# GLA with two chunks at a time and a single carried state

## The chip, the core and the metric

The kernel runs on one core of a Trainium2 chip. The core's engines work from queues of their own, each in order: PE (TensorE) does matmuls, DVE (VectorE), ACT (ScalarE) and POOL (GpSimd) do elementwise work, and SP issues most DMAs; ACT's queue issues some too. The metric is the device time of one execution, in microseconds (us), the median of three runs.

## What is computed

Two layers of a mixer with three branches (attention, RWKV-7, gated linear attention) on 256 tokens of 1024 channels, all in float32. The change is in gated linear attention (GLA): four heads with keys of 128 and values of 256 channels, in chunks of 64 tokens. `cum` is the running sum of the log decay inside a chunk.

```python
q_dec = q * jnp.exp(cum)
k_inv = k * jnp.exp(-cum)
k_to_end = k * jnp.exp(cum_last - cum)
attn = jnp.einsum('bnihd,bnjhd->bnhij', q_dec, k_inv)
attn = jnp.where(jnp.tril(jnp.ones((CHUNK, CHUNK), bool)), attn, 0.0)
o_intra = jnp.einsum('bnhij,bnjhv->bnihv', attn, v)
def step(state, inp):
    q_c, k_c, v_c, d_c = inp
    o_c = jnp.einsum('bihd,bhdv->bihv', q_c, state)
    state = state * d_c[..., None] + jnp.einsum('bjhd,bjhv->bhdv', k_c, v_c)
    return state, o_c
```

The output of a head is `o_intra` plus what the steps give; it is then divided by its root mean square over the 256 values, scaled, gated by a silu of `z` and projected.

## The kernel before

**Dense products.** Nearly all of PE's time goes to products with weights of 1024 rows. A weight tile of 128 x 1024 comes by a DMA from SP, ACT casts it to a high part (`hi_..`, L344), DVE subtracts for the low part (`lo_..`, L345), and PE runs three passes of 256-column matmuls for it (`dense`, L358, result `ps_..`; `dense_tok`, L371, with tokens in the partitions). The names say which weights: `gq`, `gk`, `gv`, `gz` are GLA's queries, keys, values and gate input, `gt` is the gate of the merge, `wo` an output projection, `rk`, `rr`, `rv` RWKV's.

**The RWKV chain.** Each layer does RWKV in two halves. A half begins with `gram` products (PE L574, masked by DVE into `Gm` L581), whose result goes out and back by DMAs on ACT's queue (`bd` L591, `Bb` L596) to the triangular solve on POOL: 31 steps of a `tm` multiply (L607) and an `Xb` update (L610), strictly one after another. The result leaves by `xd` (L612) and returns as `Xs` (L616), both issued on ACT's queue. Then a chain of eight chunks runs: `u` (PE L692, reads `Xs`), `vals` (DVE L696), `sp` (L702), a state (`gst` POOL L712, `ST` DVE L716). `ptok` turns a chunk's keys, which POOL prepares in `bks` (L643, L646).

**GLA** is called behind the first half's RWKV code and runs over its solve. `gla_gates` gives `e1`, `e2`, `ke` (the exponentials of the reference) and `el` (a chunk's whole decay). In `gla`, per layer: `qd` (L833), `ki` in `e2` (L837) and `kte` in `ke` (L838) are the three decayed tensors, channels in the partitions. For each 128 tokens PE turns `kte` (`pk` L847; ACT copies it to `kt` L848) and makes `pat` = `ki`^T `qd` (L850), which DVE masks into `at` (L851) for two chunks side by side. For each head, a state `S` is carried over three chunks: `kv` (PE L868, 64 tokens in either half of the rows), a copy (L871) or multiply-add (L873) on DVE. The output `po` [128 values, 256 tokens], twice per head, is a 128-column product with `at` (L880) for 128 tokens and a 64-column product with `S` (L882) for each of the chunks 1 to 3. ACT squares `po` (`gsq` L886), DVE copies it to `og` (L887), POOL adds the two halves of `gsq` (L888), and PE sums them over channels into `gss` (L144). After all heads comes `grn` (L891), turned by PE (`ptrg`) and spread by it (`gbc`); DVE scales `og` (L901), POOL multiplies it by the gate `tz` (L903), ACT and DVE split it into `ghi` and `glo` for `wo`.

**What sets the order.** The program is written in one order, and a scheduler that works at build time lays the instructions of each engine's queue out from it; the queues run in that order. The modulation of the next part (`adaw` L263 on DVE, one weight DMA each) is interleaved with the weight tiles. Small results of PE share three buffers (`ps_m`); `gss` holds one of them from the first head to the last.

Of the kernel before, what the change touches and what calls it, by code (L numbers as in the profile page):

```python
# [10 lines left out]
F32 = mybir.dt.float32  # L11
# [4 lines left out]
ALU = mybir.AluOpType  # L16
# [18 lines left out]
# Column slots of w_in, 256 columns each (see _w_in_columns).  # L35
# [7 lines left out]
# Columns of the packed per-channel parameters, one per 128 channels.  # L43
# [6 lines left out]
# Order of the column tiles of ada_w: shift and scale of the same channels side by side.  # L50
# [11 lines left out]
def _turn_pieces():  # L62
    """frac(2^k / 2 pi) for the steps of the pieces of an angle, each as a 12-bit part and the rest."""
# [13 lines left out]
def trunk(  # L77
# [45 lines left out]
    # running sums start again at every 32nd or 64th token  # L123
# [17 lines left out]
    def sums(ps, src, sel):  # L141
        """ps [128, 2, n]: sums over channels of src [128, 256 tokens], tokens in the partitions."""
        for half in range(2):
            PE.matmul(ps[:, half], src[:, half * P:(half + 1) * P], sel, start=True, stop=True)  # L144

    def to_rows(pool, src, n, nm):
        """[2 n, 256]: src [128, 2, n], given for tokens, turned and in two parts that one pass carries."""
# [12 lines left out]
    def spread(ps, rows, j, sel):  # L160
        """ps [128 channels, 256] = row j, both parts."""
        PE.matmul(ps, sel[:, j:j + 1].broadcast_to([sel.shape[0], P]), rows, start=True, stop=True)

    def spread2(ps, rows, j):
        """Row j to the first 64 channels, the next to the others."""
# [81 lines left out]
    def interleave():  # L247
        """Part of the modulation that is wanted later, between two weight transfers."""
# [5 lines left out]
    def ada_part(L, l, slots, pool=None):  # L254
        """Two columns of the modulation for each slot, 128 channels each, before its bias."""
# [12 lines left out]
    def start(L, hl, firsts, order):  # L268
        """The first layer's input and its first products of it, 128 channels at a time as their
        modulation comes in."""  # L270
# [62 lines left out]
    def weights(src, name, n=2048, pool=None, sub=None):  # L333
        """Both parts of n columns of a slot, in tiles of CHUNK columns."""
# [14 lines left out]
    def dense(ps, w, kt, i, act):  # L349
        """ps [128 columns, 256 tokens] = W[:, column tile i].T @ activations; a tile's rows side by side."""  # L350
# [945 lines left out]
```

## Time and profile before

| what | value |
|---|---|
| three runs, us | 1183.28, 1189.07, 1191.8 (median 1189.07) |
| span of the profiled execution, us | 1181.3 |
| PE busy | 1103.1 us, 93% |
| DVE, ACT, POOL busy | 68%, 49%, 40% |
| chain that ended last, by engine | PE 58%, POOL 16%, DVE 9%, DMA 8% |

All times in rows are microseconds from the start of the span of one profiled execution, unless marked ns. A row of a timeline gives start, duration, engine, line, operation, what it writes and reads, and how often. A matmul's duration is longer than the distance to the next one, since they are pipelined; the distance is what it costs. A matmul of float32 operands is two instructions. The granted clock is a share of TensorE's full 2.4 GHz; its lower level is 1.2 GHz.

### The profile page before, as it was taken

The numbers are of one execution on the slowest core, as the hardware profiler recorded it, in microseconds if no ns is written. First come the engines' busy times: TensorE is split into PE (matmuls) and PEld (weight loads), VectorE is DVE, ScalarE is ACT, GpSimd is POOL, SyncE is SP. The second block draws the span as 40 slices with busy tenths as digits, with TensorE's granted clock in tenths as the row PEclk, the third lists the DMA queues.
The fourth block names the chain that finished last, engine by engine and source line by source line (L and its number), as shares of the span: only waits on it lengthen the run. The fifth ranks groups of instructions, "written<-read, shape, count | busy, mean of one in ns | idle before, by whom it ended". The sixth has DMA issues, their size and how long they took to land.

```text
span 1181.3 us, 25207 instructions
## 1 busy us (share of the span) xinstructions
PE 1103.1 (93%) x10365; PEld 1001.9 (85%) x10365; DVE 799.6 (68%) x1220; ACT 578.8 (49%) x980; POOL 466.6 (40%) x609
## 2 busy tenths in 40 slices
PE   5799898999999599999989999899999969999997
PEld 3798887988999477999989889789899968799997
DVE  6978754766986667677665685367677665667774
ACT  4357233545547243554556834255384635446452
POOL 7955338324536643103100536523063753211210
PEclk7799998999999899999999989999999989999999
DMA  9665753465466443547654245334444542234761
GB/s 353 215 200 167 176 154 117 131 219 153 144 220 216 128 143 103 120 151 231 207 182 150 83 153 161 107 90 133 146 141 138 181 123 91 81 120 142 249 210 40
DMA packets 70066, 185.15 MB, mean 157 GB/s; under 512 B 24608, under 2 KB 25120, under 8 KB 69824
## 3 DMA queue, kind: packets, MB, share of 16 engines
q1 hardware_dynamic: 48304, 173.37, 46.3%
q10 hardware_dynamic: 21648, 10.18, 3.4%
q8 instruction: 81, 1.33, 0.5%
q14 instruction: 33, 0.27, 0.1%
HBM read 179.32 MB, written 4.20 MB: 155 GB/s over the span
## 4 chain that ended last, share of the span: by engine, by line
PE 58%; POOL 16%; DVE 9%; DMA 8%; issue 5%; ACT 4%; ACTq 1%; DVEq 0%; SPq 0%; POOLq 0%
PE ps_gt L358 10%; PE ps_wo L358 9%; POOL tm L607 5%; POOL Xb L610 5%; PE ps_rz L358 4%; PE y L371 3%; PE ps_gz L358 3%; PE ps_gq L358 2%; PE ps_mz L358 2%; PE ps_rk L358 2%; PE ps_rv L358 2%; DMA wr_wout<-in_wout_dram 2%; DMA Bb<-bd 1%; DMA adaw<-in_ada_dram 1%; PE sp L702 1%
## 5 line engine op out<-in xcount | busy, mean ns | idle before, releaser
L358 PE MATMUL ps_gt<-hhi,lo_gt 128*128 128x256 f32 x384 | 109.9, 286 | 0.1
L358 PE MATMUL ps_gt<-hhi,hi_gt 128*128 128x256 f32 x384 | 109.7, 286 | 0.0
L358 PE MATMUL ps_gt<-hlo,hi_gt 128*128 128x256 f32 x384 | 109.0, 284 | 0.0
L345 DVE TENSOR_TENSOR lo_gt<-wr_gt,hi_gt 128x1024 fp32r<-128x1024 f32 x48 | 63.4, 1322 | 40.1 <-ACT hi_gt L344 39.6
L345 DVE TENSOR_TENSOR lo_wo<-wr_wo,hi_wo 128x1024 fp32r<-128x1024 f32 x48 | 67.2, 1399 | 31.3 <-ACT hi_wo L344 31.1
L263 DVE SCALAR_TENSOR_TENSOR adaw<-adaw,cb 128x1024 f32<-128x1024 f32 x48 | 70.7, 1476 | 15.1 <-DMA adaw<-in_ada_dram 14.8
L344 ACT CAST hi_gt<-wr_gt 128x1024 fp32r<-128x1024 f32 x48 | 50.4, 1049 | 54.9 <-PE ps_gt L358 20.1
L344 ACT CAST hi_wo<-wr_wo 128x1024 fp32r<-128x1024 f32 x48 | 50.4, 1050 | 51.0 <-PE ps_gt L358 25.1
L358 PEld LDWEIGHTS ps_gt<-hhi,lo_gt 128*128 128x128 f32 x384 | 73.4, 191 | 1.5 <-DVE lo_gt L345 0.4
L358 PEld LDWEIGHTS ps_gt<-hhi,hi_gt 128*128 128x128 f32 x384 | 73.6, 192 | 1.0 <-issue 0.2
L712 POOL TENSOR_TENSOR gst<-ST,GC 64x256 f32<-64x256 f32 x48 | 39.0, 813 | 88.8 <-DVE ST L716 75.0
L358 PEld LDWEIGHTS ps_gt<-hlo,hi_gt 128*128 128x128 f32 x384 | 73.5, 191 | 0.6 <-issue 0.2
L607 POOL TENSOR_TENSOR tm<-Xb,Bb 128x126 f32<-128x126 f32 (+22 forms) x124 | 64.8, 523 | 22.9 <-DMA Bb<-bd 13.7
L785 POOL TENSOR_TENSOR merged<-merged,tg 128x512 f32<-128x512 f32 x14 | 24.6, 1758 | 122.6 <-DVE tg L784 108.9
L610 POOL TENSOR_TENSOR Xb<-Xb,tm 128x126 f32<-128x126 f32 (+22 forms) x124 | 61.0, 492 | 9.5
L643 POOL COPY bks<-vs 128x128 f32<-128x128 f32 x32 | 11.1, 346 | 131.4 <-PE ptok L650 125.4
L654 ACT COPY vals<-ptok 32x128 f32<-32x128 f32 x128 | 32.9, 257 | 46.7 <-PE ptok L650 34.2
L344 ACT CAST hi_gz<-wr_gz 128x1024 fp32r<-128x1024 f32 x16 | 16.8, 1048 | 50.6 <-PE ps_gz L358 18.8
L696 DVE COPY vals<-u 32x128 f32<-32x128 f32 x128 | 36.5, 286 | 7.0 <-PE u L692 5.1
L371 PE MATMUL ps_gv<-hi_gv,hhi 128*128 128x256 f32 x128 | 36.5, 289 | 3.4 <-ACT hi_gv L344 2.3
L358 PE MATMUL ps_gz<-hhi,hi_gz 128*128 128x256 f32 x128 | 39.6, 309 | 0.0
L358 PE MATMUL ps_gz<-hhi,lo_gz 128*128 128x256 f32 x128 | 39.3, 307 | 0.0
(492 smaller groups left out, 4358.9 us busy)
## 6 DMA issues: line engine op xcount, KB each, us to landing
adaw<-in_ada_dram SPq DMA_DIRECT2D x48, 512.0 KB, 3.8
wr_gt<-in_win_dram SPq DMA_DIRECT2D x48, 512.0 KB, 3.9
wr_wo<-in_wo_dram SPq DMA_DIRECT2D x48, 512.0 KB, 3.8
wr_rk<-in_win_dram SPq DMA_DIRECT2D x16, 512.0 KB, 5.1
wr_rr<-in_win_dram SPq DMA_DIRECT2D x16, 512.0 KB, 4.5
wr_rv<-in_win_dram SPq DMA_DIRECT2D x16, 512.0 KB, 4.2
wr_gv<-in_win_dram SPq DMA_DIRECT2D x16, 512.0 KB, 4.4
wr_gz<-in_win_dram SPq DMA_DIRECT2D x16, 512.0 KB, 4.2
```

Source lines behind the costliest of these rows:

```text
L263: V.scalar_tensor_tensor(w, w, 0.5, cb, ALU.mult, ALU.mult, accum_out=L.mod[:, ADA_ORDER[2 * s + i]:ADA_ORDER[2 * s + i] + 1],)
L344: A.copy(hi, wr)
L345: (sub or V).tensor_sub(lo, wr, hi.bitcast(F32))
L358: PE.matmul(ps if len(a.shape) == 2 else ps.rearrange("p (a b) -> p a b", a=2), wt[:, at + k * P:at + (k + 1) * P], a, start=i == 0, stop= ...
L371: PE.matmul(ps, a[:, st * P:(st + 1) * P] if len(a.shape) == 2 else a[:, st], wt[:, k * n % CHUNK:k * n % CHUNK + n], start=i == 0, stop=i ...
L607: G.tensor_mul(tv, Xb[:, 0:nr, m:m + 1].broadcast_to([P, nr, w]), Bb[:, m:m + 1, m + 1:32].broadcast_to([P, nr, w]))
L610: G.tensor_add(Xb[:, 0:nr, m + 1:32], Xb[:, 0:nr, m + 1:32], tv)
L654: A.copy(vals[ch % 2][rows(g2, 1 - gh), :, gh, g2], pt[32 * g:32 * g + 32, 2].rearrange("p (q v) -> p q v", q=2))
L696: V.tensor_copy(val[rows(g2, gh), :, gh, g2], u[rows(g2, gh)])
L702: PE.matmul(sp[chan(qi), 2 * gh:2 * gh + 2].rearrange("p g v -> p (g v)"), tk[:, gh, chan(qi)], val[:, qi, gh].rearrange("p g v -> p (g v) ...
L712: G.tensor_mul(gst[chan(qi)], ST[chan(qi), :, qi], R.GC[chan(qi), :, ch:ch + 1].broadcast_to([64, 4, 64]))
L785: (V if b == 2 and s == 3 else G).tensor_add(m, m, tg)
```

## The change

In each 128 tokens the queries of the second chunk now read the first chunk's keys directly: `pax` (64 keys x 64 queries, from `kte` and `qd`) fills the corner of `at` that the mask left at zero, copied there by ACT. With that only one state is needed, that of the first 128 tokens at their end: `ks` holds their keys decayed to token 128 (the first chunk's times the second chunk's decay `el`), and `qs` the queries of tokens 128 to 255 (the last chunk's times the third's decay). Both are made by four new POOL operations into a tile `far`. Only `ks` is turned, `kv` is one product over 128 rows per head, `S` a copy, and `po` three 128-column products for each of its halves.

```diff
@@ -837,18 +837,33 @@
             V.tensor_mul(e2[:, g2], e2[:, g2], ps)
             V.tensor_mul(ke[:, g2], ke[:, g2], ps)
         ki, kte = e2, ke
+
+
+        el3 = el.rearrange("p (h c) -> p h c", c=4)
+        far = gp.tile([P, 2, 4, P], F32, tag="g4", name="far", bufs=6)
+        ks, qs = far[:, 0], far[:, 1]
+        G.tensor_mul(ks[:, :, 0:64], kte[:, :, 0:64], el3[:, :, 1:2].broadcast_to([P, 4, 64]))
+        G.tensor_copy(ks[:, :, 64:128], kte[:, :, 64:128])
+        G.tensor_copy(qs[:, :, 0:64], qd[:, :, 128:192])
+        G.tensor_mul(qs[:, :, 64:128], qd[:, :, 192:256], el3[:, :, 2:3].broadcast_to([P, 4, 64]))
         at = gp.tile([P, 2, 4, P], F32, tag="g4", name="at", bufs=6)
-        kt = gp.tile([P, 2, 4, P], F32, tag="g4", name="kt", bufs=6)
         for st in range(2):
             ts = slice(st * P, (st + 1) * P)
-            pk = ps_m.tile([P, 4, P], F32, tag="m", name="pk")
             pa = ps_m.tile([P, 4, P], F32, tag="m", name="pat")
-            for hd in range(4):
-                PE.transpose(pk[:, hd], kte[:, hd, ts], ident)
-            A.copy(kt[:, st], pk)
+            px = ps_m.tile([64, 4, 64], F32, tag="m", name="pax")
             for hd in range(4):
                 PE.matmul(pa[:, hd], ki[:, hd, ts], qd[:, hd, ts], start=True, stop=True)
+            for hd in range(4):
+                PE.matmul(
+                    px[:, hd], kte[:, hd, st * P:st * P + 64], qd[:, hd, st * P + 64:(st + 1) * P],
+                    start=True, stop=True)
             V.tensor_mul(at[:, st], pa, amask.unsqueeze(1).broadcast_to([P, 4, P]))
+            A.copy(at[0:64, st, :, 64:128], px)
+        kt = gp.tile([P, 4, P], F32, name="kt")
+        pk = ps_m.tile([P, 4, P], F32, tag="m", name="pk")
+        for hd in range(4):
+            PE.transpose(pk[:, hd], ks[:, hd], ident)
+        A.copy(kt, pk)
         og = [big(f"og{i}") for i in range(2)]
         ss = ps_m.tile([P, 2, 4], F32, tag="m", name="gss")
         for hd in range(4):
@@ -861,27 +876,16 @@
                     dense_tok(ps[:, st], w, KD, 256, h, st)
                 v = gp.tile([P, 2, T], F32, tag="v", name="v", bufs=2)
                 A.copy(v, ps)
-            S = [None]
-            for ch in range(3):
-                kv = ps_m.tile([P, T], F32, tag="m", name="kv")
-                r = slice(64 * (ch % 2), 64 * (ch % 2) + 64)
-                PE.matmul(kv, kt[r, ch // 2, hd], v[r, ch // 2], start=True, stop=True)
-                Sn = gp.tile([P, T], F32, tag="S", name="S", bufs=4)
-                if ch == 0:
-                    V.tensor_copy(Sn, kv)
-                else:
-                    V.scalar_tensor_tensor(Sn, S[ch], el[:, 4 * hd + ch:4 * hd + ch + 1], kv, ALU.mult, ALU.add)
-                S.append(Sn)
+            kv = ps_m.tile([P, T], F32, tag="m", name="kv")
+            PE.matmul(kv, kt[:, hd], v[:, 0], start=True, stop=True)
+            S = gp.tile([P, T], F32, tag="S", name="S", bufs=2)
+            V.tensor_copy(S, kv)
             po = ps_m.tile([P, 2, T], F32, tag="m", name="po")
             for dt in range(2):
                 dc = slice(dt * P, (dt + 1) * P)
-                for st in range(2):
-                    first = max(1, 2 * st)
-                    PE.matmul(po[:, dt, st * P:(st + 1) * P], v[:, st, dc], at[:, st, hd], start=True, stop=False)
-                    for ch in range(first, 2 * st + 2):
-                        PE.matmul(
-                            po[:, dt, 64 * ch:64 * ch + 64], S[ch][:, dc],
-                            qd[:, hd, 64 * ch:64 * ch + 64], start=False, stop=ch == 2 * st + 1)
+                PE.matmul(po[:, dt, 0:P], v[:, 0, dc], at[:, 0, hd], start=True, stop=True)
+                PE.matmul(po[:, dt, P:T], v[:, 1, dc], at[:, 1, hd], start=True, stop=False)
+                PE.matmul(po[:, dt, P:T], S[:, dc], qs[:, hd], start=False, stop=True)
             sq = small("gsq")
             A.activation(sq, po, AF.Square)
             V.tensor_copy(og[hd // 2][:, 2 * (hd % 2):2 * (hd % 2) + 2], po)
```

Some comments fall away elsewhere, without effect on the program. SP's order of DMAs is the same. The scheduler lays the queues out anew from `pat` on; three places of the new order follow, each with rows of before first. The three are of layer 0.

DVE, behind the last of `lo_gv` before the solve, before:

```order
L345 TENSOR_TENSOR lo_gv_2290<-wr_gv_2291,hi_gv_2289 128x1024
L851 TENSOR_TENSOR at<-pat,cs 128x512
L263 SCALAR_TENSOR_TENSOR adaw_0_2471,mod_1697<-adaw_0_2471,cb 128x1024
L851 TENSOR_TENSOR at<-pat,cs 128x512
L871 COPY S<-kv 128x256
L581 TENSOR_TENSOR Gm<-gram,cs 128x4x128 x2
L873 SCALAR_TENSOR_TENSOR S<-S,el,kv 128x256
L263 SCALAR_TENSOR_TENSOR adaw_0_2474,mod_1697<-adaw_0_2474,cb 128x1024
L873 SCALAR_TENSOR_TENSOR S<-S,el,kv 128x256
```

and now:

```order
L345 TENSOR_TENSOR lo_gv_2265<-wr_gv_2266,hi_gv_2264 128x1024
L860 TENSOR_TENSOR at<-pat,cs 128x512 x2
L263 SCALAR_TENSOR_TENSOR adaw_0_2434,mod_1697<-adaw_0_2434,cb 128x1024
L581 TENSOR_TENSOR Gm<-gram,cs 128x4x128 x2
L263 SCALAR_TENSOR_TENSOR adaw_0_2437,mod_1697<-adaw_0_2437,cb 128x1024
L345 TENSOR_TENSOR lo_gz_2358<-wr_gz_2359,hi_gz_2357 128x1024
L581 TENSOR_TENSOR Gm<-gram,cs 128x4x128 x2
```

Both `at` multiplies stand ahead of the first `adaw` product, and the updates of `S` are gone.

POOL, the end of the solve, before (the two rows of a step are `tm` and `Xb`):

```order
L607 TENSOR_TENSOR tm<-Xb,Bb 128x45
L610 TENSOR_TENSOR Xb<-Xb,tm 128x15x3
L607 TENSOR_TENSOR tm<-Xb,Bb 128x30
L610 TENSOR_TENSOR Xb<-Xb,tm 128x15x2
L607 TENSOR_TENSOR tm<-Xb,Bb 128x16
L610 TENSOR_TENSOR Xb<-Xb,tm 128x16
L888 TENSOR_TENSOR gsq<-gsq 128x256
L643 COPY bks<-vs_742 128x128
```

and now:

```order
L607 TENSOR_TENSOR tm<-Xb,Bb 128x45
L610 TENSOR_TENSOR Xb<-Xb,tm 128x15x3
L607 TENSOR_TENSOR tm<-Xb,Bb 128x30
L907 TENSOR_TENSOR og_2001<-og_2001,tz 128x512
L610 TENSOR_TENSOR Xb<-Xb,tm 128x15x2
L907 TENSOR_TENSOR og_2001<-og_2001,tz 128x512
L607 TENSOR_TENSOR tm<-Xb,Bb 128x16
L907 TENSOR_TENSOR og_2002<-og_2002,tz 128x512
L610 TENSOR_TENSOR Xb<-Xb,tm 128x16
L907 TENSOR_TENSOR og_2002<-og_2002,tz 128x512
L643 COPY bks<-vs_742 128x128
L646 TENSOR_TENSOR bks<-BK_744,GC_745 128x256
```

Three of the four `og` multiplies (L907, L903 before) stand between the last steps, the fourth right behind them; the `gsq` add that stood behind the solve is now in its middle, four `gsq` adds in all standing ahead of the first `og`.

PE, around the first `u`, before:

```order
L358 MATMUL ps_gz_2625<-hhi_98,hi_gz_2619 128x256
L358 MATMUL ps_gz_2625<-hlo_99,hi_gz_2619 128x256
L358 MATMUL ps_gz_2625<-hhi_98,lo_gz_2620 128x256
L153 MATMUL ptrg_2381<-cs,hlg_2378 8x128 x2
L692 MATMUL u<-zs,Xs 32x64 x8
L644 MATMUL ptok<-cs,bks 128x128
L650 MATMUL ptok<-cs,bks 128x128 x2
L358 MATMUL ps_gz_2625<-hhi_98,hi_gz_2619 128x256
L358 MATMUL ps_gz_2625<-hlo_99,hi_gz_2619 128x256
L358 MATMUL ps_gz_2625<-hhi_98,lo_gz_2620 128x256
L358 MATMUL ps_gt_2698<-hhi_98,hi_gt_2680 128x256
L358 MATMUL ps_gt_2698<-hlo_99,hi_gt_2680 128x256
```

and now:

```order
L358 MATMUL ps_wo_2787<-ghi_2350,hi_wo_2775 128x256
L358 MATMUL ps_wo_2787<-glo_2352,hi_wo_2775 128x256
L358 MATMUL ps_wo_2787<-ghi_2350,lo_wo_2776 128x256
L358 MATMUL ps_wo_2787<-ghi_2350,hi_wo_2775 128x256
L692 MATMUL u<-zs,Xs 32x64 x8
L644 MATMUL ptok<-cs,bks 128x128
L650 MATMUL ptok<-cs,bks 128x128 x2
L358 MATMUL ps_wo_2787<-glo_2352,hi_wo_2775 128x256
L358 MATMUL ps_wo_2787<-ghi_2350,lo_wo_2776 128x256
L358 MATMUL ps_wo_2787<-ghi_2349,hi_wo_2781 128x256
L358 MATMUL ps_wo_2787<-glo_2351,hi_wo_2781 128x256
```

Here `u` reads what the solve gives. 96 `gt`, 22 `wo`, four `gbc` and three more `gz` matmuls now stand ahead of it that stood behind it. In the other layer, 19 more `gz` matmuls stand ahead of the first `u`, and on POOL two of the new `far` operations stand inside the solve.

## Rows read from the trace of the kernel before

**Rows 1.** The page, busy time, share of the span and instructions of one engine:
```profile
PE 1103.1 (93%) x10365; PEld 1001.9 (85%) x10365; DVE 799.6 (68%) x1220; ACT 578.8 (49%) x980; POOL 466.6 (40%) x609
```

**Rows 2.** Windows: busy of PE, PEld, DVE, ACT, POOL; granted clock; DMA share; GB/s:
```profile
100.00:125.00 25.00, 22.94 (x186) 22.24 (x186) 24.23 (x30) 16.55 (x24) 14.95 (x12) 1.00 0.41 128
200.00:220.00 20.00, 17.15 (x142) 15.58 (x140) 9.75 (x20) 11.69 (x19) 6.54 (x16) 0.83 0.35 105
240.00:260.00 20.00, 20.00 (x247) 18.12 (x246) 13.71 (x22) 9.20 (x14) 5.26 (x6) 1.00 0.71 221
740.00:760.00 20.00, 15.67 (x116) 13.22 (x115) 6.66 (x11) 4.43 (x7) 11.96 (x27) 0.91 0.37 105
```

**Rows 3.** Waits in 139:152, 160:210 and 735:760: total us, times, longest:
```profile
PE kv L868 <- DVE at L851: 3.1, 2, 2.0
...
PE gss L144 <- POOL gsq L888: 5.2, 2, 2.8
...
PE gss L144 <- POOL gsq L888: 4.3, 1, 4.3
```

**Rows 4.** Windows, the stretch 154 to 156:
```profile
154.00:156.00 2.00, 2.00 (x59) 1.88 (x52) 2.00 (x4) 0.00 (x0) 0.00 (x0) 0.52 0.16 20
```

**Rows 5.** Timeline of PE: start, us, engine, line, operation, count, [idle before it <-releaser]:
```profile
150.51 0.70 PE L868 MATMUL kv<-v,kt 64*128 64x256 f32 x2 [2.04 <-DVE at L851]
```

**Rows 6.** Timeline of PE in both layers, pitches and groups:
```profile
164.75 0.70 PE L868 MATMUL kv<-v,kt 64*128 64x256 f32 x4
...
727.73 1.05 PE L850 MATMUL pat<-qd,e 128*128 128x128 f32 x8
728.71 0.70 PE L868 MATMUL kv<-v,kt 64*128 64x256 f32 x4
...
760.70 0.70 PE L868 MATMUL kv<-v,kt 64*128 64x256 f32 x2
761.33 0.39 PE L358 MATMUL ps_gz<-hhi,lo_gz 128*128 128x256 f32 x1
...
762.75 0.28 PE L358 MATMUL ps_gz<-hlo,hi_gz 128*128 128x256 f32 x1
...
763.90 0.49 PE L880 MATMUL po<-at,v 128*128 128x128 f32 x2
...
766.27 0.70 PE L868 MATMUL kv<-v,kt 64*128 64x256 f32 x2
```

**Rows 7.** Timeline of DVE, layer 0:
```profile
148.62 1.23 DVE L263 SCALAR_TENSOR_TENSOR adaw<-adaw,cb 128x1024 f32<-128x1024 f32 x1 [3.17 <-DMA adaw<-in_ada_dram]
```

**Rows 8.** Timeline of POOL, layer 0, in and behind the solve:
```profile
180.73 0.72 POOL L888 TENSOR_TENSOR gsq<-gsq 128x256 f32<-128x256 f32 x1
...
203.46 0.23 POOL L610 TENSOR_TENSOR Xb<-Xb,tm 128x16 f32<-128x16 f32 x1
...
214.90 0.62 POOL L646 TENSOR_TENSOR bks<-BK,GC 128x256 f32<-128x256 f32 x1
```

**Rows 9.** Timelines of DVE and POOL, layer 0, ahead of the solve:
```profile
114.20 0.68 DVE L519 TENSOR_TENSOR ks<-ks,kam 128x512 f32<-128x512 f32 x1
...
117.16 1.79 DVE L519 TENSOR_TENSOR ks<-ks,kam 128x512 f32<-128x512 f32 x1
...
116.13 2.27 POOL L552 TENSOR_TENSOR BK<-ks,E 128x512 f32<-128x512 f32 x1
```

**Rows 10.** Timelines: PE at three first `u`, ACT's queue at one `xd`:
```profile
213.68 0.43 PE L692 MATMUL u<-zs,Xs 32*32 32x64 f32 x16
...
758.35 0.43 PE L692 MATMUL u<-zs,Xs 32*32 32x64 f32 x16
...
957.80 0.34 ACTq L612 DMA_DIRECT2D xd<-Xb  x1
...
965.68 0.65 PE L692 MATMUL u<-zs,Xs 32*32 32x64 f32 x16 [8.99 <-DMA Xs<-xd]
```

**Rows 11.** One line's instructions, L903: ns min/median/max, first and last start:
```profile
L903 POOL TENSOR_TENSOR og<-og,tz x8: 1276/1457/2275, 217.9 to 802.3; 128x512 f32<-128x512 f32 x8
```

## Prediction

> **What bounds the kernel now.** I read the page's busy shares first: PE is busy 1103.1 of 1181.3 us [rows 1]. An average does not say that PE is full everywhere, so next come the windows: in the stretch 240 to 260, inside the first layer's second half, PE is busy 20.00 of 20 [rows 2]. There a matmul fewer is its pitch less. The change lies elsewhere, where the GLA branch runs over the first triangular solve: 139 to 216 in layer 0, 715 to 780 in layer 1. There PE is not full: 17.15 of 20 in 200 to 220 and 15.67 in 740 to 760 [rows 2], and the waits name what ends last: `gss` waits for POOL's `gsq` add, 5.2 us in two stalls in layer 0 and 4.3 in one in layer 1; `kv` waits for DVE's `at`, 3.1 in two [rows 3]. Behind the longer stalls the clock falls: granted 0.83 over 200 to 220 [rows 2], and 0.52, nearly all at the lower of its two levels, 1.2 GHz, in 154 to 156 after `kv` had waited 2.04 [rows 4, 5]. So this region has two prices, the work itself and the waits with the clock behind them; and it ends in a point, the first `u` of the RWKV chain, that needs the solve's result.
>
> **Matmul work, per layer.** From rows where PE runs at full clock without waiting: one `kv` (a matmul in two instructions) starts at 760.70 and what follows it at 761.33: 0.63 us. Twelve dense 256-column matmuls start from 761.33 to 762.75, one every 0.13 at most; I take 0.12, since the first step there is a longer one. One head's output block `po` (four 128-column, six 64-column matmuls) runs 763.90 to 766.27, that is 2.37. Four `pat` matmuls run 727.73 to 728.71, 0.98, so 0.25 for one of 128 columns [rows 6].
> - `kv`: twelve become four. But two neighbours in opposite row halves ("x4" at 728.71) last 0.70 from start to end like a single one ("x2" at 760.70) [rows 6]. Layer 0 has one such pair (at 164.75), so it pays for 11 and will pay for 4: 7 x 0.63 = 4.4. Layer 1 has two such rows: 6 x 0.63 = 3.8.
> - `po`: six 128-column matmuls per head, 6 x 0.27 = 1.65 instead of 2.37: 0.7 a head, 2.8 a layer.
> - four transposes fewer, half a `pat` group: 0.5. Eight new `pax` of 64 columns: the six 64-column ones in the `po` block take (2.37 - 4 x 0.27)/6 = 0.21 each: 1.6 at most; a cheaper case is 0.17, I take 1.4.
> Sum: -6.3 in layer 0, -5.7 in layer 1, -12.0 in all.
>
> One rule speaks against the first item. The Trainium skill, "TensorEngine Tiling (Array Packing)", section "Overview", says that contractions of 64 rows can run side by side, up to twice as fast; merging such a pair would then save nothing. The trace agrees where two stand next to each other (0.70 for both) and only there; by the rule for all twelve the saving would be 1.3 a layer instead of 4.4 and 3.8, 5.6 less in all.
>
> **DVE and ACT.** Eight state updates a layer go; one eviction of four transposes goes and two small ones come. During the solve DVE waits for PE's products more than PE for DVE, and these updates feed only `po`; I count them as nothing. Without that cover they would be under 0.68 each, the price of a multiply twice as wide [rows 9], so 5 us a layer at the very most. The order does: both `at` multiplies now stand ahead of the `adaw` product which waited 3.17 for its DMA; before, the second `at` ran behind it, and `kv` waited 2.04 [rows 5, 7]. That stall goes, and with it the lower clock after it: 0.52 over 154 to 156 cost 1 us there [rows 4]; I take 2, an estimate, for the fall before and the rise behind.
>
> **POOL.** Four new operations over 256 columns per layer. The nearest row is the `bks` multiply, 0.62 [rows 8]; four of it are 2.5 us, bounds 1.8 and 4.0 (four at the 1 us a colliding one may take). In layer 0 they fall before the solve, in 100 to 125, where DVE is busy 24.23 of 25 [rows 2]. A `ks` multiply on DVE took 0.68 alone and 1.79 beside a `BK` multiply of 2.27 on POOL [rows 9]: they slow each other by 1 us or so. PE has work of 22.94 of 25 there; I charge 1 to 1.5 us in all, 0 if PE's queue covers it, 4 if all of it reaches the path. The Trainium skill, "SBUF — State Buffer", section "SBUF: two separate sides", states a lock that one of the two holds for a whole instruction; by it the four operations could cost DVE their whole 2.5 us, inside these bounds.
>
> **The first `u`, layer 0.** Before, PE reaches it at 213.68 without waiting, while the solve's last step was at 203.46 [rows 8, 10]. In the new order 96 `gt`, 22 `wo`, four `gbc` and three `gz` matmuls stand ahead of `u` that stood behind it: 125 x 0.12 = 15.0 us of work that is no longer left after it. When does it come now? On POOL three `og` multiplies (1.28 to 2.28 us, median 1.46 [rows 11]) and one more `gsq` (0.72 [rows 8]) now stand inside the solve, the multiplies among its last steps: 203.7 + 3 x 1.3 + 0.7 = 208.3. From the issue of `xd` to a `u` that waits for it the trace shows 7.9 (957.80 to 965.68 [rows 10]); so `u` can't come before 216.4, if `xd` goes out at once at 208.5. PE's own queue comes there at much the same time: the old 213.7, plus 15.0, less 6.3 of work, less the 2.0 and 2 above, less 2 to 4 of the `gss` stalls and their clock (the four `gsq` are spread now, the last in mid-solve, so I see two stalls of 2 us in place of the 5.2, estimates both), is 214.4 to 216.4. I take 216.4: 2.7 later. Gain in layer 0: 15.0 - 2.7 = **12.3**.
>
> **Layer 1.** The `u` of this layer is at 758.35 [rows 10]. Two of the `far` operations now stand in its solve: 1.2 later. PE has 19 `gz` (2.3), `pax` (1.4) and 0.2 of `po` more ahead of it, three `kv` (1.9) and four transposes (0.5) less: 1.5 later. It waits for the later of the two, with some slip: I take 1.9. Behind it are five `kv` fewer (3.2), two 128-column and twelve 64-column `po` (3.0), 19 `gz` (2.3): 8.4. Gain 8.4 - 1.9 = **6.5**. Behind the first `u` PE runs full (240 to 260 [rows 2]), so what is taken there is time.
>
> **Sum.** -12.3 - 6.5 + 1.5 = -17.3, say -17. The second half's solves I leave at zero (fewer evictions stand before `xd` there, which could give 2). The profiled span plus 2.0 around it is 1183.3, the lowest of the three runs; the median is 5.8 above, and the difference is taken off that: 1189.07 - 17 = **1172**, own range 1168 to 1176.
>
> **Rivals.**
> *The solve sets the pace (0.26).* The `og` multiplies inside it take 2.28 instead of 1.3, the upper end of their row [rows 11], since DVE works beside them, and `u` comes 3 us later; PE waits for it and takes 3 more at the lower clock. Layer 0 keeps 6, layer 1 half its gain: -9.5 and 1.5 of contention, -8: 1181. For it: the `BK` row of 2.27 shows that POOL does get slower beside DVE [rows 9]. Against: all three would have to be at that end, and the median of eight is 1.46.
> *Slower (0.07).* The `og` multiplies wait for their inputs: the last `gss`, a square root, a turn through PE, DVE's scaling. Before, the first `og` multiply ran at 217.9 [rows 11], 14 us after the solve. The solve now stands behind it in POOL's queue, and `xd`, behind the `ghi` casts in ACT's. Each us that this is late delays `u` by one, with the lower clock by up to two. Two multiplies that wait as long as this would delay it by some 14 us. The gain is eaten when the solve ends 9 to 17 us later than 208.3; 16 to 33 later the time is 1205 (17 + 16 = 33 lost, by two a us or by one). Against: in the new order the last `gsq` is in mid-solve, some 25 steps before the first multiply, so this chain starts some 10 us earlier than before, when that add stood behind the solve.
> *More (0.08).* All stalls named in [rows 3] and their clock vanish: 8.3 and 4.3 of waits, some 8 of clock, with the 12 of work: about -27, 1162.
> *All `kv` pairs ran side by side already (0.02).* As the two in the "x4" rows [rows 6], so that six slots a layer become four: 1.3 saved instead of 4.4 and 3.8, and 1178. The other pairs have other matmuls between them. By the Trainium skill's rule named above this is what 64 rows allow.
> *It does what I sum (0.57).*
>
> **Chances and range.** This kernel can be told from unchanged at about 1%, 11.9 us. Faster by more: the likeliest and "more", less some of the first's upper end: 0.64. Within 1%: the solve rival and the rest, 0.29. Slower: 0.07. The range 1160 to 1187 leaves out the far ends on both sides, the slow case among them.
>
> **What would show it.** Eight `kv` in place of 24 and no wait of `kv` for `at`; the `gss` stalls at 2 us or less and windows 200 to 220 and 740 to 760 with PE nearer 20; the last solve step of layer 0 near 208 and `u` near 216, waiting under 1.5 us. Wrong if the solve ends after 212, or if `u` waits 3 us or more, or if DVE's work in 100 to 125 pushes the `gram` products back.

## The result and the profile after

The changed kernel takes 1171.16 us (median of four runs, 1169.44 to 1175.8) where the kernel before took 1188.46 beside it: a ratio of 0.9855, 95% interval 0.9823 to 0.9887, some 17 us less. The profiled execution of after has a span of 1171.0. Its page, the rows of busy time and of the chain that ended last (beside [rows 1]):

```profile
PE 1091.8 (93%) x10293; PEld 997.3 (85%) x10293; DVE 791.7 (68%) x1204; ACT 576.9 (49%) x982; POOL 467.2 (40%) x617
...
PE 60%; POOL 15%; DMA 10%; DVE 6%; ACT 4%; issue 4%; ACTq 1%; SPq 0%; DVEq 0%; POOLq 0%
```

PE is busy 11.3 us less, with the same 93%. The windows of [rows 2] and [rows 4], now:

```profile
100.00:125.00 25.00, 22.94 (x182) 21.86 (x182) 23.73 (x27) 17.70 (x25) 16.74 (x14) 1.00 0.45 133
154.00:156.00 2.00, 1.82 (x16) 1.61 (x14) 1.88 (x3) 0.00 (x0) 0.00 (x0) 1.00 0.00 0
...
200.00:220.00 20.00, 17.89 (x142) 16.96 (x141) 16.12 (x21) 8.53 (x12) 13.90 (x21) 1.00 0.54 155
...
740.00:760.00 20.00, 17.44 (x138) 16.78 (x136) 7.37 (x12) 5.63 (x10) 8.45 (x22) 0.87 0.38 114
```

and PE's waits, in the stretches 139 to 152, 160 to 224 and 715 to 760 (beside [rows 3]; in before, the two longer stretches hold no other wait of PE):

```profile
PE pax L857 <- DVE at L860: 0.8, 1, 0.8
...
PE u L692 <- DMA Xs<-xd: 3.8, 1, 3.8
PE gss L144 <- POOL gsq L892: 3.7, 1, 3.7
PE ps_wo L358 <- DVE glo L392: 1.1, 1, 1.1
PE po L888 <- DVE S L882: 1.1, 1, 1.1
...
PE pk L865 <- POOL far L846: 2.7, 1, 2.7
PE u L692 <- DMA Xs<-xd: 2.4, 1, 2.4
PE gss L144 <- POOL gsq L892: 1.8, 2, 1.6
```

`kv` waits no more and the lower clock behind it is gone (0.52 to 1.00 in 154 to 156). But the waits have not shrunk, they stand elsewhere: before, layer 0 had 8.3 us in [rows 3]; now the rows from `pax` to `po` sum to 10.5, with a wait of 3.8 for the solve's result that was not there. In layer 1, 4.3 became 6.9.

**Where the time went, by stretch.** The windows of layer 0, from its first `gram` product to the first `u`, from there to the second half's `gram`, and on to layer 1's first `gram`; before:

```profile
143.69:213.68 69.99, 61.67 (x533) 55.15 (x532) 33.81 (x49) 21.99 (x30) 36.61 (x78) 0.90 0.45 135
213.68:343.47 129.79, 129.25 (x1411) 116.35 (x1410) 103.48 (x164) 68.72 (x130) 51.01 (x50) 1.00 0.55 171
343.47:700.34 356.87, 333.39 (x3047) 305.15 (x3046) 244.01 (x383) 186.41 (x321) 119.81 (x155) 0.98 0.51 158
```

and after:

```profile
144.19:222.83 78.64, 65.91 (x621) 62.38 (x621) 45.99 (x62) 31.65 (x45) 46.73 (x81) 0.95 0.53 156
222.83:348.25 125.42, 123.52 (x1341) 110.96 (x1341) 92.24 (x153) 63.34 (x123) 40.95 (x47) 0.97 0.55 172
348.25:692.77 344.52, 326.16 (x2990) 298.45 (x2989) 236.65 (x371) 182.29 (x316) 116.53 (x149) 0.98 0.51 156
```

One execution differs from the next by several us here, so I took three of each form (the runs below that keep the old or the new GLA in that layer) and formed means. Idle is length less PE's busy time.

| stretch | old form: us (idle) | new form: us (idle) | difference |
|---|---|---|---|
| layer 0, `gram` to `u` | 69.4 (8.9) | 77.7 (11.5) | +8.2 |
| `u` to second `gram` | 129.8 (0.5) | 124.7 (1.7) | -5.1 |
| to layer 1's `gram` | 356.3 (21.8) | 349.2 (19.6) | -7.1 |
| layer 0 in all | 555.5 (31.2) | 551.6 (32.8) | -3.9 |
| layer 1, `gram` to `gram` | 205.4 (5.6) | 198.2 (6.1) | -7.1 |
| from there to the last matmul | 272.6 | 271.7 | -0.8 |

Layer 0 gained 5.5 us of busy time and gave 1.6 back as idle. I had expected 6 to 8 us of stalls and lower clock to vanish ahead of `u`; the idle time there rose by 2.6.

**What of it is matmul work.** PE's busy time also holds the granted clock: a pair of `kv` side by side took 0.63 us to the start of the next matmul at full clock (728.71 in before), and 1.16 where the granted clock was 0.5 (746.53). After again went through the stretch from the second half's `gram` to layer 1's as follows, beside the last window above:

```profile
347.18:700.23 353.05, 332.49 (x2991) 304.29 (x2990) 236.58 (x373) 182.34 (x316) 118.87 (x155) 0.96 0.50 152
```

The same matmuls were busy 6.3 us longer, with the clock at 0.96 where it was 0.98. So the next table splits the time in three: busy time weighted by the granted clock (called work; an estimate, cut at each change of the clock), what the lower clock added to it, and idle time. These are means of three profiles of each form, for the whole span of two; differences are taken before rounding.

| stretch | old form: work, lower clock, idle | new form | difference |
|---|---|---|---|
| layer 0, `gram` to `u` | 55.1, 5.4, 8.9 | 63.2, 3.0, 11.5 | +8.1, -2.4, +2.6 |
| layer 0 in all | 512.2, 12.0, 31.2 | 503.3, 15.5, 32.8 | -9.0, +3.5, +1.5 |
| layer 1, `gram` to `gram` | 196.2, 3.6, 5.6 | 187.4, 4.8, 6.1 | -8.8, +1.2, +0.5 |
| whole span | 1075.7, 31.0, 77.5 | 1059.1, 35.6, 79.0 | -16.7, +4.6, +1.5 |

The work repeats within 2 us over the whole span (1076.2 and 1075.3 before, 1060.0 and 1058.1 after), and it fell by 16.7, as much as the timed runs did. Idle time did not fall (78.2 and 76.7, then 79.2 and 78.8). The lower clock added 26.9 and 35.2 us in the two profiles of before, 31.8 and 39.4 in those of after: with such a spread, two profiles cannot tell whether the change moves it.

### The profile page after: what moved, and what is told of

Same layout as the page of the kernel before. It is cut to its first block, busy times and chain, and to the rows that moved or that the text cites. A ratio compares the mean times of both kernels' runs of the same rounds, so it can differ in the third digit from the quotient of the medians.

```text
span 1171.0 us, 25069 instructions
## 1 busy us (share of the span) xinstructions
PE 1091.8 (93%) x10293; PEld 997.3 (85%) x10293; DVE 791.7 (68%) x1204; ACT 576.9 (49%) x982; POOL 467.2 (40%) x617
## 4 chain that ended last, share of the span: by engine, by line
PE 60%; POOL 15%; DMA 10%; DVE 6%; ACT 4%; issue 4%; ACTq 1%; SPq 0%; DVEq 0%; POOLq 0%
PE ps_gt L358 10%; PE ps_wo L358 9%; POOL tm L607 6%; POOL Xb L610 5%; PE ps_rz L358 4%; PE ps_rv L358 4%; PE y L371 3%; PE ps_mz L358 2%; PE ps_gq L358 2%; DMA adaw<-in_ada_dram 2%; DMA wr_wout<-in_wout_dram 2%; PE ps_cq L358 2%; DMA Bb<-bd 2%; PE ps_rr L358 2%; DMA Xs<-xd 1%
## 5 line engine op out<-in xcount | busy, mean ns | idle before, releaser
L345 DVE TENSOR_TENSOR lo_gt<-wr_gt,hi_gt 128x1024 fp32r<-128x1024 f32 x48 | 61.9, 1291 | 42.2 <-ACT hi_gt L344 41.9
L263 DVE SCALAR_TENSOR_TENSOR adaw<-adaw,cb 128x1024 f32<-128x1024 f32 x48 | 66.5, 1388 | 25.1 <-DMA adaw<-in_ada_dram 25.0
L607 POOL TENSOR_TENSOR tm<-Xb,Bb 128x126 f32<-128x126 f32 (+22 forms) x124 | 68.0, 548 | 30.3 <-DMA Bb<-bd 21.2
L712 POOL TENSOR_TENSOR gst<-ST,GC 64x256 f32<-64x256 f32 x48 | 34.8, 725 | 76.3 <-DVE ST L716 62.7
L643 POOL COPY bks<-vs 128x128 f32<-128x128 f32 x32 | 13.7, 429 | 123.6 <-PE ptok L650 106.5
L654 ACT COPY vals<-ptok 32x128 f32<-32x128 f32 x128 | 32.8, 256 | 51.8 <-PE ptok L650 32.1
L1037 POOL TENSOR_SCALAR pr<-pr,sm 128x128 f32<-128x128 f32 (+1 forms) x32 | 28.7, 911 | 27.6 <-DVE sm L1035 27.3
L358 PE MATMUL ps_gz<-hlo,hi_gz 128*128 128x256 f32 x128 | 38.4, 300 | 0.0
L371 PE MATMUL ps_gv<-hi_gv,hlo 128*128 128x256 f32 x128 | 37.2, 292 | 0.9 <-DVE hlo L392 0.9
```

What stands on the lines that cost most here:

```text
L263: V.scalar_tensor_tensor(w, w, 0.5, cb, ALU.mult, ALU.mult, accum_out=L.mod[:, ADA_ORDER[2 * s + i]:ADA_ORDER[2 * s + i] + 1],)
L345: (sub or V).tensor_sub(lo, wr, hi.bitcast(F32))
L358: PE.matmul(ps if len(a.shape) == 2 else ps.rearrange("p (a b) -> p a b", a=2), wt[:, at + k * P:at + (k + 1) * P], a, start=i == 0, stop= ...
L371: PE.matmul(ps, a[:, st * P:(st + 1) * P] if len(a.shape) == 2 else a[:, st], wt[:, k * n % CHUNK:k * n % CHUNK + n], start=i == 0, stop=i ...
L607: G.tensor_mul(tv, Xb[:, 0:nr, m:m + 1].broadcast_to([P, nr, w]), Bb[:, m:m + 1, m + 1:32].broadcast_to([P, nr, w]))
L654: A.copy(vals[ch % 2][rows(g2, 1 - gh), :, gh, g2], pt[32 * g:32 * g + 32, 2].rearrange("p (q v) -> p q v", q=2))
```

## Experiments

**Both kernels again.** No edit, to see how far runs repeat.

> The kernel before once more, for a second profile of it: ratio 1.000. Its runs spread from 1183.28 to 1191.8, and the profile is of the fastest. If the spread comes from the stalls of PE on the GLA branch's small results, a profile of a slower execution shows longer gss or kv waits or more lower clock in 140 to 220 and 735 to 760; if it comes from the solves' ends, later first u.

Before against itself: 0.9996 (0.997 to 1.0021). Its profile is 5.8 us longer than the first, with 8.3 us more of lower clock and no more idle time (76.7 and 78.2).

> The changed kernel once more, beside the one before on the same chip. By the sum of the prediction (matmul work -12.0, less time in waits, contention +1.5): -17, ratio 0.986. If the two profiles seen so far, 1181.3 and 1171.0, stand for all executions: -10, ratio 0.991. The spread of the runs then says which.

After again: 0.9862 (0.9828 to 0.9896), some 16 us less. The four profiled spans are 1181.3 and 1187.1 of before, 1171.0 and 1176.2 of after: a pair of single profiles can be off by 5 us, so totals are taken from the timed runs.

**One layer at a time.** `gla_old` is the function before.

```diff
-            gla(L, l, h, gates, merged, gp)
+            (gla if l == 0 else gla_old)(L, l, h, gates, merged, gp)
```

> The change in layer 0 alone; layer 1's GLA is computed as before, and each layer's queues keep the order of their own kernel. By my sum: -12.3 + 1.5 = -10.8 (ratio 0.991). By the two profiles: at the start of layer 1's RWKV preparation the changed kernel was only 5.0 ahead (643.16 against 648.17), so -5 (0.996). By matmul work alone: -6.3.

0.9944 (0.9921 to 0.9967): 6.7 us less, 3.9 to 9.4.

> The change in layer 1 alone. By my sum: -6.5 (ratio 0.9945). By the two profiles: between layer 1's first gram product and its second half's the changed kernel gained 1.2 (700.34 to 902.81 against 692.77 to 894.04), and another 1.5 behind it, so -1 to -3 (0.998). By matmul work alone: -5.7.

With `l == 1` in that line: 0.9912 (0.988 to 0.9943): 10.5 us less, 6.8 to 14.3. The two add up to 17.2, the whole change. My split was 10.8 (12.3 less 1.5 of contention) and 6.5; the first lies outside its interval, the second just outside. The work of the whole span, 1075.7 before, was 1067.5 and 1066.3.

**What POOL does, taken away one at a time.** The `gsq` adds to DVE (this edit takes the like-made add of another norm along):

```diff
-            G.tensor_add(sq[:, 0], sq[:, 0], sq[:, 1])
+            V.tensor_add(sq[:, 0], sq[:, 0], sq[:, 1])
```

> The changed kernel, but the gsq adds are on DVE; the new order then has neither gsq nor og multiplies inside the first solve. If the length of the solve, 42.7 us in the changed kernel against 35 before, is what holds the first u back in layer 0: the solve takes 33 to 35 (35 less two gsq of 0.7), u comes 67 to 69 us after the first gram product instead of 77 to 78 and doesn't wait; 68 matmuls (8.2 us) go back behind it; the gss stalls (3.7 and 2 to 4) and their lower clock go too: 3 to 7 us less than the changed kernel, ratio to before 0.980 to 0.984. If PE's work alone decides and waits only change places: as the changed kernel, 0.986. If DVE's added load of eight adds shows: 0.988 or more.

0.9874 (0.9847 to 0.9901). The solve was 7 us shorter (36.0 instead of 42.8) and the first `u` 10.8 us earlier after `gram`, yet the kernel was no faster. Its first `u` on PE's timeline and the window from `gram` to it:

```profile
213.97 0.65 PE L692 MATMUL u<-zs,Xs 32*32 32x64 f32 x16 [11.12 <-DMA Xs<-xd]
...
146.18:213.97 67.79, 54.31 (x552) 51.44 (x552) 37.76 (x55) 28.34 (x40) 39.92 (x71) 0.95 0.49 149
```

The scheduler had laid out fewer dense matmuls ahead of this `u` (312, not 380), and PE waited 11.12 us for it. Such an edit changes the order everywhere, not just the cost it is meant for.

The four `far` operations to DVE (`G.` to `V.` in the four lines of the diff):

> The changed kernel with the four far operations of each layer on DVE. If they cost DVE by colliding from POOL, moving them changes little in layer 0; in layer 1 they leave the solve (1.2) and the pk wait on far (0.6 to 2.7) goes: 1 to 4 less than the changed kernel, ratio 0.983 to 0.985. If DVE's load of eight more operations (0.4 to 0.7 each, in a stretch where it is 94% busy in layer 0) decides: 1 to 3 more, 0.987 to 0.989.

0.9867 (0.9834 to 0.9901).

The `og` multiplies to DVE:

```diff
-            G.tensor_mul(o, o, zs)
+            V.tensor_mul(o, o, zs)
```

> The changed kernel with the og*tz multiplies on DVE. The first solve keeps three gsq but loses its three og multiplies: 42.7 becomes 38.8 if only their own time counts, 36 if the DVE work that runs at the same time was slowed and slowing by them. 46 matmuls (5.5 us) go back behind the first u. If the solve sets u there: u 4 to 7 us earlier, so about as the changed kernel, between -2 and +2 (0.984 to 0.988). If the multiplies in the solve cost nothing because PE is the bound: PE comes to u without a wait and the time is the same; the wait at u tells the two apart.

0.9855 (0.9823 to 0.9887). All three agree with the changed kernel within their intervals: moving any of POOL's added operations to DVE, with the new order that comes of it, wins nothing. With `og` gone from it the first solve still took 40.3 us, 33.9 of them in its own steps.

**Three times the `kv` product.** The sum stays the same, since each starts anew.

```diff
-            PE.matmul(kv, kt[:, hd], v[:, 0], start=True, stop=True)
+            for _ in range(3):
+                PE.matmul(kv, kt[:, hd], v[:, 0], start=True, stop=True)
```

> The changed kernel with each of its eight kv products done three times over (the same result): 16 x 0.63 = 10.1 us of matmuls more, 5 in each layer. If matmul work counts one for one in both layers: +10 against the changed kernel, ratio to before 0.994 to 0.995. If in layer 0 the solve sets the time of u and PE waits there anyway: only layer 1's +5 and little in layer 0; in the new order the og multiplies also stand behind that solve, not inside it, so its length should be 36 to 37 instead of 42.7. Then +3 to +6, 0.989 to 0.991.

0.9908 (0.9872 to 0.9944): 6 us more than the changed kernel, give or take 6. The work of the whole span is 1064.7, 5.7 more than the mean of the changed kernel's two. PE's timeline where the three stand together, and the windows from `gram` to `u` and of all of layer 0:

```profile
152.84 1.56 PE L881 MATMUL kv<-v,kt 128*128 128x256 f32 x6
154.24 0.38 PE L887 MATMUL po<-at,v 128*128 128x128 f32 x2
...
146.45:214.54 68.09, 56.98 (x541) 53.32 (x540) 34.40 (x50) 26.08 (x37) 40.98 (x75) 0.94 0.49 147
...
146.45:696.91 550.46, 518.38 (x4967) 474.44 (x4966) 374.67 (x584) 277.62 (x481) 205.76 (x275) 0.97 0.52 159
```

The three take 1.40, 0.47 each on average, not 0.63: 16 more are some 7.5 us. The time and the work fit that, within their spread. What I did not look for says more. In this kernel the scheduler kept nearly the old order: 284 dense matmuls ahead of the first `u` (259 before, 380 after), and `u` came 68.1 us behind `gram`, as early as before. Layer 0 still took 550.5, 5 us less than the mean of the old form, with 3.8 us of extra products in it: together 8.8, as much as the 9.0 of work that the change takes out of the layer. So it does not take work moved ahead of `u` to have the gain of layer 0.

**More work ahead of the first `u`.** If the wait of 3.8 us is a loss, 26 more `wo` matmuls ahead of it should fill it. An order given at build time puts `u` of layer 0 behind the last of that group:

```diff
+    for ins in trail.pop(key, ()):
+        tc.add_manual_dep(
+            ins.ins, recent[0].ins.name,
+            mybir.DependencyInfo(mybir.DependencyClass.NoSync, mybir.DependencyReason.DATA),
+            reason="first u")
```

> The changed kernel with one order fixed by hand: the first u of layer 0 stands behind all 48 wo matmuls of the first output pair instead of 22, 26 matmuls (3.1 us) more ahead of it; solve and POOL as in the changed kernel. In three profiles PE waited 2.7 to 3.8 there. If that wait is what layer 0 loses, it falls to under 1 and the lower clock behind it goes: 3 to 5 us less than the changed kernel, ratio to before 0.982 to 0.984. If the wait costs nothing, or the work ahead of u only waits for its own inputs (glo): no change, 0.986.

0.9873 (0.9846 to 0.99). The window from `gram` to `u`:

```profile
146.80:222.76 75.96, 69.42 (x646) 65.76 (x645) 44.34 (x61) 31.82 (x45) 45.18 (x78) 0.96 0.52 157
```

`u` did not wait, and the idle time ahead of it fell to 6.5 us. Nothing was gained in the total. Two variants, with the shorter solve too: `gsq` on DVE and `u` behind all 96 `gt`, and `gsq` and `og` on DVE with `u` behind 122 `gt` and the 48 `wo`.

> The kernel with the gsq adds on DVE, with one order fixed by hand: the first u of layer 0 behind all 96 gt matmuls instead of 50, 46 (5.5 us) more ahead of it. There u came 67.8 us after the first gram product and PE waited 11.1 for it. If that wait is lost time, it becomes 5 to 6, and the time 5 to 7 less than with the gsq adds on DVE alone: ratio to before 0.981 to 0.983. If not, as that kernel, 0.987.

0.9865 (0.9833 to 0.9897).

> gsq adds and og multiplies on DVE, so that the first solve holds nothing else (33 to 36 us), and u by hand behind 122 gt and 48 wo matmuls, 120 more than with the gsq adds on DVE alone (14.4 us). If the solve's length and the wait at u are the two losses of layer 0: no wait at u, u 71 to 74 us after the first gram product with more work done ahead of it than in any kernel so far: 10 to 13 us less than with the gsq adds on DVE alone, ratio to before 0.976 to 0.979. If DVE, with twelve operations more a layer, becomes the bound there: waits for its lo parts and for glo, and 0.984 or more.

0.9864 (0.9824 to 0.9904). In both, `u` ran without waiting (0.2 us and none), and the total stayed.

**Where that gain went.** With the later `u` the second half's solve began 23.7 us behind its `gram`, against 16.3 in the changed kernel: on DVE the second pair of mask multiplies of that half had come behind other work, 10.0 us after `gram` instead of 6.0. The rows where each pair starts, of the run with the later `u` (L590 there is L581 of after) and of after:

```profile
360.01 0.69 DVE L590 TENSOR_TENSOR Gm<-gram,cs 128x512 f32<-128x512 f32 x1
```

```profile
354.26 1.27 DVE L581 TENSOR_TENSOR Gm<-gram,cs 128x512 f32<-128x512 f32 x2
```

So I put DVE's scaling of `cx` in layer 0 behind that pair:

```diff
-                for s in range(npair):
+                with (tc.issue_after(last_gm[0].ins) if l == 0 else ExitStack()):
+                    for s in range(npair):
```

> As the run with the later first u of layer 0 (0.9873; its second solve began 23.7 us behind the second gram product, against 16.3 to 17.3 in the changed kernel), with one thing more: in layer 0 DVE runs the scaling of cx (eight products and the splits behind them) behind the last Gm of the second half instead of ahead of it, so that Bb and the second solve can begin earlier. Theory A: what the later u won went into the later second solve. Then the solve begins 17 to 19 us behind gram, its stall (products for the queries waiting for DVE, 7 to 11 us) shrinks by 3 to 5 us, the time falls by as much: 1168 to 1172 where before is 1190, ratio 0.982 to 0.985. Theory B: the end of layer 0 is set by the amount of DVE and chain work in the second half as a whole, not by that solve's start: the ratio stays at 0.986 to 0.988, and the stall comes back at another place.

0.9884 (0.9863 to 0.9906): theory B. The solve began 3 us sooner (20.5 behind `gram`), and the stall at the end of it did not shrink. PE's largest waits in 340 to 425, with the later `u`, then with this edit on top:

```profile
PE ps_uk L367 <- DVE rotb L942: 6.6, 1, 6.6
PE sc L1032 <- POOL kr L999: 5.0, 1, 5.0
```

```profile
PE ps_uv L380 <- DVE rotb L942: 7.6, 1, 7.6
PE sc L1033 <- POOL kr L1000: 6.4, 1, 6.4
```

**All of layer 0, side by side.** From first `gram` to layer 1's `gram`, by windows of one profile each; the dense matmuls ahead of `u` are counted in the program's order.

| kernel | dense ahead of `u` | `gram` to `u` | wait of `u` | layer 0 | PE busy | idle |
|---|---|---|---|---|---|---|
| before | 259 | 70.0 | 0 | 556.7 | 524.3 | 32.3 |
| before again | 259 | 69.3 | 0.4 | 556.1 | 523.5 | 32.5 |
| change in layer 1 only | 259 | 69.0 | 0.2 | 553.8 | 525.0 | 28.8 |
| `kv` three times | 284 | 68.1 | 3.9 | 550.5 | 518.4 | 32.1 |
| `gsq` on DVE | 312 | 67.8 | 11.1 | 547.8 | 513.1 | 34.7 |
| `far` on DVE | 315 | 66.4 | 3.3 | 548.1 | 514.4 | 33.7 |
| `og` on DVE | 334 | 70.0 | 3.9 | 548.9 | 514.7 | 34.3 |
| `gsq` on DVE, `u` behind 96 `gt` | 358 | 69.9 | 0.2 | 550.8 | 515.4 | 35.4 |
| after | 380 | 78.6 | 3.8 | 548.6 | 515.6 | 33.0 |
| after again | 380 | 77.3 | 2.7 | 554.2 | 521.3 | 32.9 |
| change in layer 0 only | 380 | 77.2 | 3.6 | 551.9 | 519.5 | 32.4 |
| later `u` | 406 | 76.0 | 0 | 547.0 | 516.2 | 30.9 |
| later `u`, `Gm` early | 406 | 77.0 | 0.8 | 550.4 | 515.3 | 35.1 |
| `gsq`, `og` on DVE, later `u` | 432 | 82.3 | 0 | 553.1 | 517.0 | 36.2 |

Every form of the new GLA has 3 to 11 us less of busy time than the mean of the old (524.3), and none has clearly less idle. Between 284 and 432 dense matmuls ahead of `u`, layer 0 shows no trend.

## Why the prediction came out as it did

**The total** was right, -17.3 for a measured -17, and so was the chance on faster by more than 1%: the interval of 0.9823 to 0.9887 lies below 0.99. The way there was not, and the hit was luck in part. Layer 0 gave 4 us less than my sum and layer 1, by the timed runs, 4 more. The sum was -12.0 of matmul work, +1.5 of contention and, for the rest, -6.8 of stalls, lower clock and overlap; the profiles show -16.7 of work, no contention that PE felt, and no fall in idle time.

**The matmul work** was summed too small: 6.3 and 5.7, where the work fell by 9.0 and 8.8 (the busy time, with the clock in it, by 5.5 and 7.6). By the distance from each to the next matmul, put to full clock, `kv` and `po` together came to 15.7 us before and 7.0 after in layer 0, and to 15.0 and 6.7 in layer 1: 8.7 and 8.3 less, 7.2 and 6.6 summed. The new `kv` is followed after 0.25 to 0.54 at full clock (0.63 priced), and the new `po` block costs 1.4 a head (1.65 priced). The rest is spread over other products, whose neighbours changed; some 1 us of layer 1's is eight matmuls that now lie behind its window. Eight `kv` stand in the trace, and none waits for `at`. (Eight `pax` by my own step are 1.7 us at most, not 1.6; in layer 1 they cost 1.4, as taken.)

**The step that failed is "the first `u`, layer 0".** I put 15.0 us of work ahead of it and let it come 2.7 later, for a gain of 12.3. Behind `u`, 12.2 of the 15.0 did come out (5.1 and 7.1 in the table of stretches). But `u` came 8.2 later. By my own two routes to its time:

*The solve* ended at 212.70, not 208.3. POOL's timeline in it, and DVE's beside:

```profile
203.21 2.49 POOL L610 TENSOR_TENSOR Xb<-Xb,tm 128x70 f32<-128x70 f32 x1
...
207.40 1.29 POOL L907 TENSOR_TENSOR og<-og,tz 128x512 f32<-128x512 f32 x1
...
208.85 1.30 POOL L907 TENSOR_TENSOR og<-og,tz 128x512 f32<-128x512 f32 x1
210.12 0.67 POOL L607 TENSOR_TENSOR tm<-Xb,Bb 128x16 f32<-128x16 f32 x1
210.75 1.31 POOL L907 TENSOR_TENSOR og<-og,tz 128x512 f32<-128x512 f32 x1
212.00 0.70 POOL L610 TENSOR_TENSOR Xb<-Xb,tm 128x16 f32<-128x16 f32 x1
...
203.15 2.36 DVE L345 TENSOR_TENSOR lo_gt<-wr_gt,hi_gt 128x1024 fp32r<-128x1024 f32 x2
```

The three `og` multiplies took 1.3 each, as priced; the rival's 2.28 was wrong. What I missed are the solve's own steps: their 62 durations sum to 32.97 us, against 29.62 before (32.5 and 33.1 in the other two profiles of the new form, 27.8 and 28.9 of the old), and the start was 1.6 later. Here one step of 70 elements, whose neighbours take 0.3, ends just after two DVE subtractions, and the last `Xb` took 0.70 where it took 0.23 in [rows 8]. With the gate's work moved into the solve, DVE's came along: 16.12 busy in 200 to 220, from 9.75 [rows 2]. The Trainium skill, "SBUF — State Buffer", section "SBUF: two separate sides", says that a POOL operation, or a DVE operation with two inputs in SBUF, holds the ports that they share for its whole length while the other waits; the step of 2.49 agrees with that, over two such DVE operations in a row. I had weighed this for the four new operations, and not for the solve's steps.

*From `xd` to `u`* it took 10.1 us, not the 7.9 of [rows 10]. The queue of ACT, PE's first `u`, and the DMA row of that stretch (KB each, median us to landing):

```profile
212.73 0.34 ACTq L612 DMA_DIRECT2D xd<-Xb  x1
214.96 1.39 ACTq L616 DMA_DIRECT2D Xs<-xd  x2
...
222.83 0.65 PE L692 MATMUL u<-zs,Xs 32*32 32x64 f32 x16 [3.80 <-DMA Xs<-xd]
...
Xs<-xd ACTq DMA_DIRECT2D x2, 128.0 KB, 6.4
...
216.00:223.00 7.00, 2.06 (x23) 1.69 (x25) 4.63 (x7) 2.15 (x3) 0.00 (x0) 0.97 1.00 275
```

While `Xs` was under way the DMA engines were full (share 1.00, 275 GB/s), with weights from SP.

*PE's own queue* was to get there at 214.4 to 216.4 because 6 to 8 us of stalls and lower clock would go. Without its last wait it got there at 219.0. That part is where the sum really broke. The work ahead of `u` grew by 8.1, as summed (15.0 less 6.3), and the lower clock gave back 2.4; but moving work ahead of `u` is a gain only as far as it fills idle time, and the idle time ahead of `u` went from 8.9 to 11.5. The test I had named, that the solve ends after 212 or `u` waits 3 us or more, was met on both counts.

Still, the late `u` is not what cost the rest: with the wait gone (the later `u`), or `u` as early as before (284 to 334 in the table), layer 0 stayed at 547 to 553. What is shown is that layer 0's gain is matmul work taken out (9.0 us), less what lower clock and idle time took back (5.0 in the mean of three profiles), and that PE's 31 to 36 us of idle time came back in other places. What fixes that amount is not settled; the start of the second solve alone is not it.

**Layer 1.** The steps held: `u` came 62.5, 61.5 and 60.4 us behind `gram` where it came 58.0, 59.8 and 61.9 (1.6 later; 1.9 said), though with a new wait for `far` of 2.7 in one profile, 0.6 in another and none in the third. From `u` to the second half's `gram`:

```profile
758.35:902.81 144.46, 144.46 (x1523) 129.66 (x1522) 102.39 (x159) 78.95 (x140) 51.02 (x56) 1.00 0.40 126
```

before, and after

```profile
755.31:894.04 138.73, 138.47 (x1453) 125.28 (x1453) 97.73 (x150) 75.57 (x137) 48.97 (x55) 0.96 0.41 125
```

The means of three are 145.4 and 136.7: 8.7 less, 8.4 said. By work it was 10.6 less, of which the lower clock took back 1.7. Here PE runs full behind `u`, so matmuls saved are time saved. By the timed runs layer 1 gave 10.5, by the profiles 7.9; the difference lies within the interval, and I can't place it.

**POOL's four operations** in layer 0 cost 4.9 us of its time, above my upper bound of 4.0:

```profile
114.85 0.86 POOL L847 COPY far<-qd 128x256 f32<-128x256 f32 x1
115.68 1.05 POOL L848 TENSOR_TENSOR far<-qd,el 128x256 f32<-128x256 f32 x1
...
127.68 1.57 POOL L845 TENSOR_TENSOR far<-ke,el 128x256 f32<-128x256 f32 x1 [4.38 <-DVE ke L838]
129.20 1.39 POOL L846 COPY far<-ke 128x256 f32<-128x256 f32 x1
```

and none of PE's that shows: 22.94 of 25 busy in 100 to 125 both times. Only two of the four ran in that stretch, where I had put all; the other two came at 127.68 and 129.20. The first `gram` came at 144.19, 146.00 and 144.96 with the new form in layer 0, at 143.69, 146.11 and 150.06 with the old: no later. The 1.5 us charged was not seen.

**The rivals.** "The solve sets the pace" had layer 0 right (6 us kept) by a mechanism that was half right: the result was late, by stretched steps and a slow landing, not by dear multiplies; layer 1 contradicts it. "Slower" needed a solve 9 us past 208.3; it was 4.4. "More" fell with the stalls that stayed; its own terms add up to 32.6, not 27. Had the old `kv` pairs run side by side, 6.4 us of matmul work would have gone instead of 12.0; in the two layers' stretches the busy time fell by 13.1 and the work by 17.8.

## What to carry to other kernels

Work moved ahead of a wait is worth what it fills of idle time, not its own length: write down the idle time that is to vanish, row by row, and ask what will be late next. What paid here was matmul work removed, in both layers. Busy time holds the clock: weighted by it, the work of two executions of one kernel agreed within 2 us where the busy times differed by 6 or 7. And where a scheduler lays out the program, every small edit gives a new order: compare busy and idle time over a whole layer, in several profiles, before a stall is blamed.

## What the hardware showed that I had not expected

- POOL's short steps stretch when some of DVE's operations run beside them: a step of 0.3 us took 2.49, and the sum over a solve rose from 29.62 to 32.97. All four solves of all fourteen profiles have 3472 steps. The 1583 with no DVE operation beside them took at most 0.04 us more than the shortest of their kind and size. Of the others 615 took over 0.3 us more, and each of these ended within 0.33 us behind the end of a DVE operation. Where a `lo_` subtraction was under way as the step began, it took 0.92 us more on average; where `at` was, 0.005.
- One pair of 128 KB loads, `Xs` of layer 0, landed after 6.4 and 5.8 us in two profiles of the changed kernel; the median of all eight loads was 3.0 in the profile of before, but 4.7 in its repeat. In after, weights filled the DMA engines meanwhile; that these are the cause was not tested. The Trainium skill, "DMA: Bandwidth & Descriptors", section "Latency and other measured facts", says that memory latency rises with load; the row agrees in direction.
- Three `kv` over 128 rows took 1.40 us, 0.47 each; a single one was followed after 0.25 by a dense matmul, after 0.44 to 0.54 by a `po`. Behind one over 64 rows of the same width the next matmul, dense or `gram`, started after 0.63 at full clock [rows 6]. What makes the difference was not tried.
